# Layer norms behind the convolutions in channel layout, with their statistics sent through DRAM

## The chip, the cores and the metric

One core of one Trainium2 chip runs the whole program. The time is device time in microseconds (us) from the start to the end of one execution, median over the runs.

Engines in the listings: PE multiplies matrices (TensorE), DVE is the vector engine, ACT the scalar engine, POOL the GpSimd engine, SP the queue from which nearly all DMAs are issued. PE writes its results to PSUM, which has eight banks here; all other operands lie in SBUF. A DMA moves data between SBUF and DRAM.

## What is computed

One layer of a hybrid encoder, for a prompt of 512 tokens and a sample of 1024 tokens with shared weights. The part that the change touches is the layer norm behind the depthwise convolution:

```python
def _layernorm(x, g, b):
    mu = jnp.mean(x, axis=-1, keepdims=True)
    xc = x - mu
    return xc * lax.rsqrt(jnp.mean(xc * xc, axis=-1, keepdims=True) + EPS) * g + b
...
z = rmsnorm(x, norm_attn_g) @ w_in
a_out = window_attn(q, k, v, bias, band, sink)           # 8 heads of 64
c = ca * sigmoid(cb)                                     # 512 channels
c = dwconv(c, conv_dw_w, conv_dw_b)                      # 31 taps
c = silu(layernorm(c, conv_ln_g, conv_ln_b))             # mean over the 512 channels of a token
x = x + concat([a_out, c], axis=-1) @ w_out
...
```

What follows (a gated feed-forward network with a 3-tap convolution, and a last norm) isn't touched.

## The kernel before

Tokens are cut into blocks of 128: the prompt has blocks 0 to 3, the sample blocks 4 to 11. Every large product is done with operands split into a high and a low part, three matmuls of 128x512 per product (hi x hi, hi x lo, lo x hi); L317 to L319 are those of the projections, L813 to L815 those of the out projection, each with one line number for each of the three.

The projected channels lie with channels on the 128 partitions and tokens along the row, so that the convolution can shift along the tokens. The 512 channels are four chunks. The layer norm wants the mean over channels, which here lie across partitions. `conv_norm(i)` (L744) therefore turns each block: four PE transposes (L760) bring it to 128 tokens x 512 channels in a PSUM bank, `bn_stats` and `bn_aggr` (L765, L766) on DVE give mean and variance of each token, two small operations on POOL (L147, L148) make rstd of the variance, one DVE operation (L769) subtracts and multiplies with a value per partition, and four more PE transposes (L775) bring the block back. Then ACT applies g and b per channel (L781, four activations of 128x128), tanh (L782), DVE finishes the swish (L783), and ACT and DVE make the high and low parts (L784, L785) that the out projection reads as kc 4 to 7. The attention's half of the concatenation is kc 0 to 3. `out_half(i, n)` (L803) does block i's out projection, half n, in a PSUM bank, with kc 0 to 7 in order.

For the prompt, `prompt_attention` goes through the attention units 0 to 7 (two per block; `scores` with L655 to L676, `values` with L697 to L723) and does the norm of block u - 4 behind unit u. All chunks of the convolution are kept in SBUF (`kept`). `prompt_out` waits for each block through the set `ready`. For the sample, the convolution's result went through DRAM (`cvd`) and each block is read back into `held`; the norms of blocks 4 and 5 run inside `sample()` next to the feed-forward network of the prompt, and those of blocks 6 to 11 after it.

What sets the order: the code is written as generators that are advanced in turn at paces (`pace`, `side`), and a scheduler then orders the instructions on each engine, which executes its queue strictly in order. Buffers are named slots (`Slots`): letters h, q, d, c, s for SBUF, a, u, b, c for PSUM banks, and a new tile takes the slot that was freed first among the smallest that fit, so a change in one place gives other slots, and other waits, further on. From about 733 us on the order is written out by hand; the change doesn't reach there.

Other lines that the prediction uses: L407 to L433 (`evac`) empty the projections' PSUM banks on DVE, L433 for q, L407 for the convolution's gate; L435 and L438 make the low part of q and write both parts to DRAM (`qsd`), from where they are read back (h<-qsd); L659 is the softmax's first step on DVE, L700, L721 and L723 make low parts and sums of the attention on DVE and POOL, L699, L719 and L720 copy from PSUM on ACT; L983 (DVE), L1005 (DVE) and L1007 (SP, write to gap) belong to the feed-forward network beside it; L152 loads rows of x, and L1116 loads norm_ffn_g to all partitions.

## Time and profile before

| | |
|---|---|
| median of 3 runs | 1481.91 us (1481.87 to 1482.33) |
| profiled execution | 1484.05 us |
| its span on the core | 1482.1 us |
| mean granted clock of PE | 0.998 |
| instructions | 19791 |
| DVE, ACT, POOL busy | 75%, 54%, 54% |

The profile is of one execution. A row of the timeline gives the start, the length, the engine, the line, the tiles written and read and, in brackets, how long the engine had been idle and what released it. Matmuls are pipelined: one of 128x512 takes 0.39 us but they start 0.23 us apart, so a row's length is no cost by itself; the distance between starts is. A group's row gives the busy time and the mean of one, then the idle time ahead of its instructions with its releasers. A row of DMA issues gives the size of one in KB and the median time from issue to landing.

### The profile page before, as it was taken

What the parts mean: (1) busy time and instruction counts of PE and PEld (TensorE: products, weight loads), DVE (VectorE), ACT (ScalarE), POOL (GpSimd) and SP (SyncE); (2) the same over time, 40 slices, a digit from 0 to 9 for tenths busy, and PEclk for the clock granted to TensorE, in tenths of its full rate; (3) what the DMA queues carried; (4) which work ended last, traced back from release to release, by engine and by line L of the source; (5) the groups of instructions that cost most, each with busy time, mean ns of one, the idle gap of its engine ahead of it and who ended that gap; (6) DMA issues with size and microseconds to landing.
All of it is one profiled execution on the core that took longest, in us unless ns stands there. A gap on an engine that the chain in (4) does not pass through costs nothing.

```text
span 1482.1 us, 19791 instructions
## 1 busy us (share of the span) xinstructions
PE 1464.6 (99%) x6688; PEld 1206.0 (81%) x6688; DVE 1117.9 (75%) x1502; ACT 805.8 (54%) x1434; POOL 803.8 (54%) x696
## 2 busy tenths in 40 slices
PE   9999999999999999999999999999999999999998
PEld 7788887878888888788887888888888888888886
DVE  6877945658998989666598888888886846578873
ACT  7534555458778677644565445444454553433355
POOL 3555453328888776422566666666655341135555
PEclk9999999999999999999999999999999999999999
DMA  9555331744444464373214433333333494356744
GB/s 368 191 152 145 110 101 36 244 161 142 122 142 135 136 192 136 110 282 123 84 58 142 150 129 127 131 124 123 123 126 96 147 337 152 125 190 220 228 166 156
DMA packets 124625, 228.17 MB, mean 154 GB/s; under 512 B 20420, under 2 KB 45764, under 8 KB 124397
## 3 DMA queue, kind: packets, MB, share of 16 engines
q1 hardware_dynamic: 124092, 226.37, 46.4%
q8 instruction: 52, 0.85, 0.2%
q10 hardware_dynamic: 432, 0.56, 0.1%
q14 instruction: 49, 0.39, 0.1%
HBM read 166.83 MB, written 61.10 MB: 154 GB/s over the span
## 4 chain that ended last, share of the span: by engine, by line
PE 88%; DVE 4%; DMA 2%; ACT 2%; issue 2%; POOL 1%; SPq 0%; POOLq 0%; ACTq 0%; DVEq 0%
PE w L1249 8%; PE w L1250 8%; PE w L1251 8%; PE w L1613 7%; PE w L1614 7%; PE w L1612 7%; PE b L317 4%; PE u L317 4%; PE b L318 4%; PE u L318 4%; PE u L319 4%; PE b L319 4%; PE a L655 1%; PE a L697 1%; PE u L813 1%
## 5 line engine op out<-in xcount | busy, mean ns | idle before, releaser
L164 POOL TENSOR_TENSOR q<-q,q 128x1024 fp32r<-128x1024 f32 x64 | 154.4, 2413 | 69.4 <-ACT q L163 48.7
L1102 POOL TENSOR_TENSOR q<-q,q 128x512 fp32r<-128x512 f32 x82 | 125.4, 1538 | 115.2 <-ACT q L1235 115.2
L1102 DVE TENSOR_TENSOR h<-h,h 128x512 fp32r<-128x512 f32 (+1 forms) x161 | 132.6, 854 | 55.9 <-ACT h L1110 23.7
L1612 PE MATMUL w<-h,h 128*128 128x512 f32 x432 | 168.0, 389 | 0.0
L1614 PE MATMUL w<-h,h 128*128 128x512 f32 x432 | 168.0, 389 | 0.0
L1613 PE MATMUL w<-h,h 128*128 128x512 f32 x412 | 160.3, 389 | 0.0
L1102 POOL TENSOR_TENSOR h<-h,h 128x512 fp32r<-128x512 f32 (+1 forms) x46 | 67.9, 1478 | 141.7 <-ACT h L1595 119.6
L1249 PE MATMUL w<-h,q 128*128 128x512 f32 x350 | 137.7, 393 | 1.1 <-ACT w L1320 0.9
L1251 PE MATMUL w<-h,q 128*128 128x512 f32 x350 | 136.4, 390 | 0.1
L1250 PE MATMUL w<-h,q 128*128 128x512 f32 x350 | 136.3, 389 | 0.0
L1110 ACT CAST h<-h 128x512 fp32r<-128x512 f32 x116 | 69.2, 620 | 106.0 <-DVE h L1102 30.5
L317 PE MATMUL b<-h,q 128*128 128x512 f32 x312 | 123.2, 395 | 1.5 <-ACT h L466 0.9
L318 PE MATMUL b<-h,q 128*128 128x512 f32 x312 | 122.8, 393 | 0.0
L319 PE MATMUL b<-h,q 128*128 128x512 f32 x312 | 122.6, 394 | 0.0
L317 PE MATMUL u<-h,q 128*128 128x512 f32 x272 | 107.3, 395 | 0.8 <-DVE h L983 0.8
L319 PE MATMUL u<-h,q 128*128 128x512 f32 x272 | 107.2, 394 | 0.0
L318 PE MATMUL u<-h,q 128*128 128x512 f32 x272 | 107.2, 394 | 0.0
L357 DVE SCALAR_TENSOR_TENSOR c<-d,cvw,c 128x512 f32<-128x512 f32 x128 | 95.8, 749 | 1.5
L163 ACT CAST q<-q 128x1024 fp32r<-128x1024 f32 x66 | 69.0, 1046 | 49.0 <-PE b L318 13.3
L1612 PEld LDWEIGHTS w<-h,h 128*128 128x128 f32 x432 | 81.1, 188 | 16.9
L1614 PEld LDWEIGHTS w<-h,h 128*128 128x128 f32 x432 | 81.1, 188 | 16.6
L348 POOL TENSOR_TENSOR h<-h,h 128x512 f32<-128x512 f32 x62 | 82.1, 1326 | 20.9 <-ACT h L347 16.6
(501 smaller groups left out, 4011.1 us busy)
## 6 DMA issues: line engine op xcount, KB each, us to landing
q<-in_laid_w_up SPq DMA_DIRECT2D x88, 512.0 KB, 3.8
ga<-q SPq DMA_DIRECT2D x65, 256.0 KB, 2.2
h<-gap SPq DMA_DIRECT2D x57, 256.0 KB, 3.8
h<-ga SPq DMA_DIRECT2D x57, 256.0 KB, 3.5
h<-in_w_down SPq DMA_DIRECT2D x52, 256.0 KB, 3.5
q<-in_laid_w_in SPq DMA_DIRECT2D x22, 512.0 KB, 4.0
gap<-h SPq DMA_DIRECT2D x42, 256.0 KB, 2.6
q<-in_x_sample SPq DMA_DIRECT2D x15, 512.0 KB, 7.7
```

What stands on the lines that cost most here:

```text
L164: (nc.vector if dve else nc.gpsimd).tensor_tensor(lo[:], raw[:], hi[:].bitcast(F32), op=ALU.subtract)
L317: nc.tensor.matmul(out, whi[:, kc, :], hi[:], start=(kc == 0), stop=False)
L318: nc.tensor.matmul(out, whi[:, kc, :], lo[:], start=False, stop=False)
L319: nc.tensor.matmul(out, wlo[:, kc, :], hi[:], start=False, stop=(kc == KC - 1))
L357: nc.vector.scalar_tensor_tensor(acc[:], src(t), w(t), acc[:], op0=ALU.mult, op1=ALU.add)
L1102: (eng or nc.vector).tensor_tensor(out, a, b, op=ALU.subtract)
L1249: nc.tensor.matmul(out, whi[:, s], hi[:], start=(start and c == 0), stop=False, **go)
L1250: nc.tensor.matmul(out, whi[:, s], lo[:], start=False, stop=False, **go)
L1251: nc.tensor.matmul(out, wlo[:, s], hi[:], start=False, stop=(stop and c == 3), **go)
L1612: nc.tensor.matmul(out, sh[:, c], th[:], start=(p == 0 and not seeded), stop=False, **go)
L1613: nc.tensor.matmul(out, sh[:, c], tl[:], start=False, stop=False, **go)
L1614: nc.tensor.matmul(out, sl[:, c], th[:], start=False, stop=(p == NPAIR - 1), **go)
```

## The change

The turn back goes away. Blocks stay in channel layout, and only the statistics, one mean and one rstd per token, are brought to a form that can be applied there: a row along the tokens, the same on all partitions.

For a block of the sample the four transposes for the statistics stay. rstd is made in place beside the mean (`spread_stats`), both are written to a small DRAM tensor `lnd` (2 x 128 values, in single elements), and a second DMA reads them back broadcast to all partitions (128 x 256). DVE subtracts the mean's row from the block as loaded (128x512, `held`), POOL multiplies with the rstd's row, and ACT reads that in place of the PSUM bank.

For the prompt the norms of all four blocks are done together, behind unit 4: 16 transposes, four times `bn_stats` and `bn_aggr`, one rstd for all (128 x 4), one write of 128 x 8 values to `pstat`, and two broadcast reads of 128 x 512. Then the work goes by channel chunks, 512 tokens at a time: chunks 0 and 1 behind unit 5, 2 and 3 behind unit 6, each with a subtraction on DVE, a multiplication on POOL, and the same operations as before on whole chunks (one activation in place of four). The out projection reads slices of the chunks (`Chunks`). The four blocks become ready together, behind unit 6.

In the core of the diff, line numbers shift: transposes for the statistics are L769 in the changed kernel (L913 for the prompt), the write and the read of `lnd` L748 and L750, the prompt's subtractions L929, and L832 to L834 are what L813 to L815 were.

```diff
@@ -741,6 +741,15 @@
         for L in range(2):
             nc.sync.dma_start(cats[i, 0][L][:].bitcast(F32), catd[blocks[i][1], :, L, :].rearrange("p (j t) -> p j t", t=P))
 
+    lnd = [dr.tile([2, P], F32, name=f"lnd{b}") for b in range(8)]
+
+    def spread_stats(b, mv):
+        rstd_of(mv[:, 1:2], 1.0, mv[:, 1:2])
+        nc.sync.dma_start(lnd[b][:].rearrange("s p -> p s"), mv[:])
+        wide = sb.tile([2, P])
+        nc.sync.dma_start(wide[:], lnd[b][:].partition_broadcast(P))
+        return wide
+
     def conv_norm(i):
         G, b = blocks[i]
         if G["g"] == 0:
@@ -760,25 +769,35 @@
             nc.tensor.transpose(pt[:, c * P:(c + 1) * P], cv[c], ident[:])
         if G["g"] == 0 and b == G["nb"] - 1:
             kept.clear()
-        held = None
-        st, mv, rs = sm(6), sm(2), sm(1)
+        st, mv = sm(6), sm(2)
         nc.vector.bn_stats(st[:], pt[:])
         nc.vector.bn_aggr(mv[:], st[:])
-        rstd_of(mv[:, 1:2], 1.0, rs[:])
-        xh = sb.tile([CCH])
-        nc.vector.tensor_scalar(xh[:], pt[:], mv[:, 0:1], rs[:], op0=ALU.subtract, op1=ALU.mult)
-        del pt
-        for _ in range(YN):
-            yield 0.0
-        p2 = bank("norm")
-        for c in range(4):
-            nc.tensor.transpose(p2[:, c * P:(c + 1) * P], xh[:, c * P:(c + 1) * P], ident[:])
+        if G["g"] == 1:
+            del pt
+            wide = spread_stats(b, mv)
+            for _ in range(YN):
+                yield 0.0
+            nc.vector.tensor_tensor(held[:], held[:], wide[:, 0:1, :].to_broadcast([P, 4, P]), op=ALU.subtract)
+            nc.gpsimd.tensor_tensor(held[:], held[:], wide[:, 1:2, :].to_broadcast([P, 4, P]), op=ALU.mult)
+            del wide
+            p2 = held[:].rearrange("p c t -> p (c t)")
+        else:
+            rs, xh = sm(1), sb.tile([CCH])
+            rstd_of(mv[:, 1:2], 1.0, rs[:])
+            nc.vector.tensor_scalar(xh[:], pt[:], mv[:, 0:1], rs[:], op0=ALU.subtract, op1=ALU.mult)
+            del pt
+            for _ in range(YN):
+                yield 0.0
+            p2 = bank("norm")
+            for c in range(4):
+                nc.tensor.transpose(p2[:, c * P:(c + 1) * P], xh[:, c * P:(c + 1) * P], ident[:])
         y, t = sb.tile([4, P]), sb.tile([4, P])
         for c in range(4):
             o, n = y[:, c, :], p2[:, c * P:(c + 1) * P]
             if G["g"] == 1:
                 o, n = o.rearrange("p (k h) -> p h k", h=2), n.rearrange("p (h k) -> p h k", h=2)
             nc.scalar.activation(o, n, AF.Identity, scale=lng[:, c:c + 1], bias=lnb[:, c:c + 1])
+        held = None
         nc.scalar.activation(t[:], y[:], AF.Tanh)
         nc.vector.scalar_tensor_tensor(t[:], t[:], 1.0, y[:], op0=ALU.add, op1=ALU.mult)
         nc.scalar.copy(cat[0][:], t[:])
@@ -882,13 +901,64 @@
     use.update(step="b", turn="a", attn="au", norm="au", out="u", gate="b")
 
     ready = set()
-
-    def normed(i):
-        yield from conv_norm(i)
-        ready.add(i)
+    pstat = dr.tile([4, 2, P], F32, name="pstat")
+    wides = []
+
+    def prompt_stats():
+        drain(convs)
+        mv = sm(8)
+        for b in range(4):
+            pt = bank("norm")
+            for c in range(4):
+                nc.tensor.transpose(pt[:, c * P:(c + 1) * P], kept[c][:, b * P:(b + 1) * P], ident[:])
+            st = sm(6)
+            nc.vector.bn_stats(st[:], pt[:])
+            nc.vector.bn_aggr(mv[:, 2 * b:2 * b + 2], st[:])
+            del pt
+            yield 0.0
+        var = mv[:].rearrange("p (b s) -> p b s", s=2)[:, :, 1]
+        nc.gpsimd.tensor_scalar(var, var, 1.0, EPS, op0=ALU.mult, op1=ALU.add)
+        nc.gpsimd.tensor_tensor(var, var, nhalf[:], op=ALU.pow)
+        nc.sync.dma_start(pstat[:].rearrange("b s p -> p (b s)"), mv[:])
+        for s in range(2):
+            wides.append(sb.tile([4, P]))
+            nc.sync.dma_start(wides[s][:], pstat[:, s, :].partition_broadcast(P))
+
+    def prompt_norm(c):
+        x = kept.pop(c)
+        nc.vector.tensor_tensor(x[:], x[:], wides[0][:].rearrange("p b t -> p (b t)"), op=ALU.subtract)
+        nc.gpsimd.tensor_tensor(x[:], x[:], wides[1][:].rearrange("p b t -> p (b t)"), op=ALU.mult)
+        yield 0.0
+        hi, lo, t = sb.tile([NT], F32R), sb.tile([NT], F32R), sb.tile([NT])
+        nc.scalar.activation(x[:], x[:], AF.Identity, scale=lng[:, c:c + 1], bias=lnb[:, c:c + 1])
+        nc.scalar.activation(t[:], x[:], AF.Tanh)
+        nc.vector.scalar_tensor_tensor(t[:], t[:], 1.0, x[:], op0=ALU.add, op1=ALU.mult)
+        nc.scalar.copy(hi[:], t[:])
+        nc.vector.tensor_tensor(lo[:], t[:], hi[:].bitcast(F32), op=ALU.subtract)
+        for i in range(4):
+            for full, part in zip(cats.setdefault((i, 1), (Chunks(i), Chunks(i))), (hi, lo)):
+                full.parts.append(part)
+        yield 0.0
+
+    class Chunks:
+        def __init__(self, i):
+            self.parts, self.cols = [], slice(i * P, (i + 1) * P)
+
+        def __getitem__(self, at):
+            return self.parts[at[1]][:, self.cols]
+
+    def in_turn(*gens):
+        for gen in gens:
+            yield from gen
+
+    def all_ready():
+        wides.clear()
+        ready.update(range(4))
+        yield 0.0
 
     def prompt_attention():
-        yield from attention(0, 8, {u: normed(u - 4) for u in range(4, 8)})
```

Three places in the order. Names are kind of slot, slot number and a running number; "h41_1051" is a tile in SBUF slot h41, "c0_343" one in PSUM bank c0.

The first is DVE in the prompt's part, around units 4 to 6. Before, from the evacuation of q (L433, bank b0_91) on:

```order
L433 SCALAR_TENSOR_TENSOR h34_358_2223<-b0_91_2163,d1_125_569 128x512
L765 BN_STATS s18_352_2194<-a2_92_2189 128x6
L700 TENSOR_TENSOR d0_339_2095<-u1_87_2089,h35_338_2094 128x512
L670 RECIPROCAL s17_325_2011<-s17_325_2011 128x4
L766 BN_AGGR s19_353_2195<-s18_352_2194 128x2
L700 TENSOR_TENSOR h30_344_2127<-u0_90_2121,h38_343_2126 128x512
L659 ISA h29_367_2266,s21_365_2261<-u1_95_2263,q11_186_1099,nsink_81 128x256
L659 ISA s21_365_2261 128x1
L407 TENSOR_TENSOR d0_371_2314<-b1_94_2252,h0_109_467 128x512
L721 TENSOR_TENSOR h38_349_2158<-a1_88_2098,h36_331_2061 64x512
L700 TENSOR_TENSOR q10_375_2339<-u1_101_2333,q4_374_2338 128x512
L407 TENSOR_TENSOR q7_378_2374<-b0_100_2326,d1_125_569 128x512
```

and in the changed kernel, directly behind the four blocks' statistics and an L721 that writes h38_349; L433 with bank b0_91 is again the evacuation of q, h14_361 is the broadcast row of the means, and L407 with b1_95 empties the bank that b1_94 was:

```order
L659 ISA d0_370_2323,s23_364_2285<-u1_100_2320,q12_187_1101,nsink_81 128x256
L659 ISA s23_364_2285 128x1
L659 ISA h32_366_2290,s23_364_2285<-a1_97_2287,q11_186_1099,nsink_81 128x256
L659 ISA s23_364_2285 128x1
L700 TENSOR_TENSOR q9_372_2348<-u0_102_2342,h44_371_2347 128x512
L433 SCALAR_TENSOR_TENSOR h38_355_2233<-b0_91_2172,d1_125_569 128x512
L700 TENSOR_TENSOR q10_374_2363<-a1_103_2357,q4_373_2362 128x512
L929 TENSOR_TENSOR h2_83_354<-h2_83_354,h14_361_2279 128x512
L929 TENSOR_TENSOR h27_141_744<-h27_141_744,h14_361_2279 128x512
L929 TENSOR_TENSOR h17_198_1177<-h17_198_1177,h14_361_2279 128x512
L929 TENSOR_TENSOR h26_291_1817<-h26_291_1817,h14_361_2279 128x512
L407 TENSOR_TENSOR h38_368_2311<-b1_95_2255,h0_109_467 128x512
```

L433 moved from ahead of the first statistics to behind the softmax steps L659 and two low parts; its tile h38_355 takes the slot that the POOL sum behind L721 (h38_349) frees. The four subtractions stand ahead of L407. The row of L659 with only a sum as its output fetches the accumulated sum of the one before.

The second is PE at block 5 of the sample. Before: the turn back (L775) of block 5, and its first use as h13 and h56 in bank u1_349:

```order
L813 MATMUL u1_349_6600<-h21_1005_6093,h15_1063_6418 128x512
L814 MATMUL u1_349_6600<-h31_1006_6094,h15_1063_6418 128x512
L815 MATMUL u1_349_6600<-h21_1005_6093,h46_1064_6419 128x512
L775 MATMUL c0_343_6498<-ident_82,h48_1075_6455 128x128 x4
L813 MATMUL u0_350_6674<-h23_1102_6623,h57_1037_6262 128x512
L814 MATMUL u0_350_6674<-h20_1103_6624,h57_1037_6262 128x512
...
L813 MATMUL b0_352_6730<-h40_1106_6650,h15_1063_6418 128x512
L814 MATMUL b0_352_6730<-h39_1107_6651,h15_1063_6418 128x512
L813 MATMUL u1_349_6600<-h58_1012_6125,h13_1065_6422 128x512
L814 MATMUL u1_349_6600<-h10_1013_6126,h13_1065_6422 128x512
L815 MATMUL b0_352_6730<-h40_1106_6650,h46_1064_6419 128x512
```

and in the changed kernel: the transposes for the statistics, and the first use of the normed rows, h41 and h13, in bank c0_343:

```order
L712 MATMUL a1_336_6428<-q11_1057_6396,h60_431_2734 128x512
L769 MATMUL c0_334_6405<-ident_82,h43_1053_6386 128x128 x4
L711 MATMUL a1_336_6428<-q12_1061_6424,h60_431_2734 128x512
...
L834 MATMUL b0_347_6745<-h21_992_6058,h26_1107_6651 128x512
L769 MATMUL a2_348_6758<-ident_82,h58_1120_6735 128x128 x4
L832 MATMUL b1_349_6797<-h25_1087_6582,h29_1106_6650 128x512
L833 MATMUL b1_349_6797<-h46_1088_6583,h29_1106_6650 128x512
L769 MATMUL a0_345_6660<-ident_82,h33_1105_6648 128x128 x4
L834 MATMUL b1_349_6797<-h25_1087_6582,h26_1107_6651 128x512
L832 MATMUL c0_343_6559<-h54_999_6090,h41_1051_6384 128x512
L833 MATMUL c0_343_6559<-h8_1000_6091,h41_1051_6384 128x512
```

Between the last transposes of the block and its first use stood 42 rows before, all behind the turn back; now 48 rows lie between the statistics' transposes and the use, with the subtraction, the activations and the rest of the norm beside them on the other engines.

The third is SP in the same stretch of the changed kernel, from the load of block 6's convolution on. lnd1 is block 5's, lnd2 and lnd3 those of blocks 6 and 7, and in_norm_ffn_g is the load that L1116 issued before (L1186 now):

```order
L762 DMA h33_1105_6648<-cvd_159 128x512
L748 DMA lnd1_1273<-s30_1059_6411 128x2x1
L1077 DMA gap24_3279<-q11_1069_6490 128x512
L152 DMA q1_1141_6853<-in_x_sample 128x1024
L750 DMA q3_1060_6417<-lnd1_1273 128x256
L152 DMA q11_1124_6743<-in_x_sample 128x1024
L1186 DMA q3_1070_6496<-in_norm_ffn_g 128x1024
L748 DMA lnd3_1275<-s8_1126_6764 128x2x1
L748 DMA lnd2_1274<-s4_1109_6666 128x2x1
L750 DMA h32_1127_6770<-lnd3_1275 128x256
L152 DMA q14_1155_6949<-in_x_sample 128x1024
L750 DMA h59_1110_6672<-lnd2_1274 128x256
```

Before, there were no writes of statistics and no reads of them; the loads and the gap write stood there alone. Now the read of lnd1 stands behind the write to gap24 and a load of x, and the writes of blocks 6 and 7 stand behind the load of norm_ffn_g.

More of the change, by code (lines that the diff above doesn't have):

```diff
@@ L890, in prompt_attention @@
+    class Chunks:
[10 more added lines that the diff above has]
+        yield 0.0
     def prompt_attention():
-        yield from attention(0, 8, {u: normed(u - 4) for u in range(4, 8)})
+        yield from attention(0, 8, {4: prompt_stats(), 5: in_turn(prompt_norm(0), prompt_norm(1)),
+                                    6: in_turn(prompt_norm(2), prompt_norm(3), all_ready())})
```

## The prediction, on record before the changed kernel was timed

> **What bounds the kernel now.** First the page, for the engines and the chain that ended last:
>
> ```profile
> PE 1464.6 (99%) x6688; PEld 1206.0 (81%) x6688; DVE 1117.9 (75%) x1502; ACT 805.8 (54%) x1434; POOL 803.8 (54%) x696
> PE 88%; DVE 4%; DMA 2%; ACT 2%; issue 2%; POOL 1%; SPq 0%; POOLq 0%; ACTq 0%; DVEq 0%
> ```
>
> TensorE (PE) is busy 99% of the span and carries 88% of the chain: a microsecond of matmul taken away is a microsecond won, as long as PE doesn't have to wait for something new. Then the windows over the stretch in which the change reorders PE, about 217 to 731 us. The columns are window, length, busy time of PE, PEld, DVE, ACT and POOL (with counts), granted clock, DMA share, GB/s:
>
> ```profile
> 216.70:226.40 9.70, 9.55 (x49) 7.95 (x48) 5.32 (x13) 5.06 (x12) 4.36 (x7) 1.00 0.67 189
> 237.00:251.00 14.00, 12.92 (x69) 10.18 (x68) 10.33 (x22) 10.04 (x22) 5.15 (x10) 1.00 0.01 2
> 276.80:300.00 23.20, 22.88 (x104) 18.50 (x103) 14.47 (x21) 9.76 (x19) 8.03 (x8) 1.00 0.93 285
> 613.00:625.20 12.20, 9.86 (x48) 7.43 (x47) 8.53 (x15) 5.84 (x13) 2.33 (x6) 1.00 0.24 80
> 625.20:628.60 3.40, 3.39 (x9) 2.67 (x10) 3.37 (x9) 3.40 (x9) 0.19 (x1) 0.54 0.10 36
> 633.00:649.20 16.20, 16.20 (x80) 13.43 (x79) 11.06 (x19) 11.02 (x24) 2.98 (x4) 1.00 0.97 376
> 649.20:735.00 85.80, 85.80 (x418) 70.88 (x417) 51.49 (x66) 39.65 (x78) 36.99 (x43) 1.00 0.37 123
> ```
>
> From 633 us on PE has no idle time at all, and that is where blocks 5 to 11 of the sample are normed and projected. So each norm is hidden today, and the question is by how much. The stretch 613 to 625.2 has 2.3 us idle, and directly behind it the granted clock is 0.54 for 3.4 us.
>
> **What is removed.** Of the turn back, block 4's in the timeline of PE (start, length, instruction, what it waited for), with what follows:
>
> ```profile
> 620.62 0.60 PE L775 MATMUL c<-ident,h 128*128 128x128 f32 x4
> 620.98 0.48 PE L317 MATMUL u<-h,q 128*128 128x512 f32 x1
> 621.30 0.40 PE L318 MATMUL u<-h,q 128*128 128x512 f32 x1
> 621.54 0.40 PE L319 MATMUL u<-h,q 128*128 128x512 f32 x1
> 622.54 0.50 PE L655 MATMUL a<-q,h 128*128 128x256 f32 x2 [0.61 <-DVE h L721]
> ```
>
> Four transposes put the next matmul 0.36 us later, and that one delays its successor by 0.32 instead of the usual 0.23: 0.36 + 0.32 - 0.23 = 0.45 us. Twelve blocks: 12 x 0.45 = 5.4 us. This block's own four stand just ahead of a wait for DVE, whose end they don't set, so they win nothing: 4.95 us. The twelve tensor_scalars (L769) go from DVE, but as many subtractions come; DVE is off the path in all but the places below.
>
> **What is added: a round trip through DRAM for every block of the sample.** The rows for it, per issue in KB and us to landing, then groups with mean ns:
>
> ```profile
> qsd<-h SPq DMA_DIRECT2D x44, 128.0 KB, 2.4
> cvd<-h SPq DMA_DIRECT2D x8, 256.0 KB, 3.0
> h<-qsd SPq DMA_DIRECT2D x24, 256.0 KB, 3.1
> q<-in_norm_ffn_g SPq DMA_DIRECT2D x1, 512.0 KB, 7.0
> L723 POOL TENSOR_TENSOR h<-h,h 64x512 fp32r<-64x512 f32 x17 | 22.8, 1339 | 25.7 <-DVE h L721 25.4
> L148 POOL TENSOR_TENSOR s<-s,nhalf 128x1 f32<-128x1 f32 x12 | 8.6, 714 | 1.0
> ```
>
> The write of the statistics (256 elements of 4 bytes) is in no row of this kernel. Its nearest neighbours are 2.4 us (qsd) and 3.0 us (cvd, in runs of 256 bytes); I take 2.5. The broadcast read of 128 KB: below 2.4 hardly, 3.0 taken, 7.0 (the row of the broadcast norm_ffn_g, four times the bytes) as the far end, since the DMA share in its stretch is 0.97. *One rule speaks to this:* the Trainium skill, "DMA: Bandwidth & Descriptors", section "Anatomy of one DMA", has about 2.0 us fixed for each DMA plus bytes over 436 GB/s; the pair would be 4.3 us instead of 5.5, and the wait worked out below 1.2 us shorter, the sum +2.7 instead of +3.9. The rows above land later than that for small transfers, so I go by the rows.
>
> Blocks 6 to 11 have 16 to 25 us between their statistics and their first use by PE in the new order (counted at 0.23 us a matmul), against a chain of some 15 us with its queues: I put no stall there. **Block 5 is the exception.** In the new order its statistics stand 38 matmuls, eight transposes of L697 and two groups of four ahead of the first matmul that reads its normed rows (c0 with h41): 38 x 0.23 + 0.8 + 2 x 0.45 = 10.4 us. Before, the turn-back at 643.5 stood 10.0 us ahead of that use (here the first row is the statistics' transposes, the last the use), and behind it was only this chain:
>
> ```profile
> 636.92 0.60 PE L760 MATMUL c<-ident,h 128*128 128x128 f32 x4
> 643.50 0.68 DVE L1005 TENSOR_TENSOR q<-b,q 128x512 f32<-128x512 f32 x1
> 644.14 1.52 ACT L781 ACTIVATE q<-c,vecs 128x128 f32<-128x128 f32 x4 [2.97 <-PE c L775]
> 646.70 0.58 ACT L719 COPY h<-a 64x512 f32<-64x512 f32 x1
> 647.30 0.63 ACT L782 ACTIVATE q<-q 128x512 f32<-128x512 f32 x1
> 648.00 0.68 DVE L783 SCALAR_TENSOR_TENSOR q<-q,q 128x512 f32<-128x512 f32 x1
> 649.09 0.62 ACT L784 CAST h<-q 128x512 fp32r<-128x512 f32 x1
> 649.55 1.28 POOL L723 TENSOR_TENSOR h<-h,h 64x512 fp32r<-64x512 f32 x1 [5.80 <-DVE h L721]
> 649.74 1.64 DVE L785 TENSOR_TENSOR h<-q,h 128x512 fp32r<-128x512 f32 x1 [0.33 <-ACT h L784]
> 653.53 0.39 PE L813 MATMUL u<-h,h 128*128 128x512 f32 x1
> ```
>
> Laid out on the times of before: the statistics' transposes stand six matmuls later than at 636.92, and end at 638.7; bn_stats and bn_aggr, behind one tap in DVE's queue, to 641.2; the two small POOL operations 0.95 to 642.15; write 2.5 to 644.75; on SP the read stands behind a gap write, which before was issued at 644.20 behind the evacuation L1005, so it leaves at 644.8; read 3.0 to 647.8; subtraction 0.7; multiplication on POOL 1.34; four activations 1.5; tanh 0.65; two copies of the attention ahead in ACT's queue 1.1 (L719 and its like); the DVE product lies beside them; cast 0.65: 653.85. PE asks at 638.7 + 10.4 = 649.1. **Stall: 4.7 us.** If every queue were empty it is 2.7; with the read at 7.0 it is 8.7. Behind the waiting cast and the waiting read stand the copies and casts of later blocks on ACT, and on SP the x loads and the reads of blocks 6 and 7, which have the slack just named.
>
> After such a stall I expect the clock drop seen at 625.2: 3.4 us at 0.54 cost 3.4 x 0.46 = 1.6 us. It came there behind 2.3 us of idle time in several pieces; the 1.1 us idle in 237 to 251 left the clock at 1.00. So 4.7 us should be enough, and 1.6 us is the term (0 is the other end).
>
> **What is moved in the prompt.** All four blocks' statistics are now taken after unit 4, in one bunch, and the rows of DVE that follow are in another order:
>
> ```profile
> 219.59 0.69 DVE L433 SCALAR_TENSOR_TENSOR h<-b,d 128x512 f32<-128x512 f32 x1
> 226.98 1.24 SPq L438 DMA_DIRECT2D qsd<-d  x2
> 230.10 0.69 DVE L407 TENSOR_TENSOR d<-b,h 128x512 f32<-128x512 f32 x1 [3.79 <-DMA qsd<-d]
> ```
>
> L433, which empties bank b0, ran at 219.59 with slack. Now it takes a slot that L723 frees, and stands behind L659, which writes the d slot that the two qsd writes hold until 230.1 less some tenths. L659 twice, one L700 and L433 itself bring it to about 231.7, while PE, which from the last statistics (226.9) to the projection that wants b0 has 2.0 us of work, asks at 228.9: **2.75 us** of stall (2.0 to 3.3). Then the round trip: statistics done 227.9, POOL 1.0, write 3.0, read 3.1, so 235.1. Four subtractions and L407, which empties bank b1, take 5 x 0.69, to 238.6; PE asks for b1 24 matmuls and one score after 231.9, at 237.7: 0.9 us. But the subtractions read two SBUF tensors while POOL multiplies, and L785 above took 1.64 instead of about 0.69 where it met L723; with two such meetings of 1 us it is 2.9. I take **1.9 us**. *This is the second rule:* the Trainium skill, "SBUF — State Buffer", section "SBUF: two separate sides", calls the port pair of the two engines an exclusive lock held for the whole instruction; by it alone the term is 2.9, without it 0.9, and the row at 649.74 agrees with the lock. On the other side the turn of units 6 and 7 with the old waits goes: idle time 0.15 + 1.08 + 0.32 in the first three windows, and some four restarts at 0.39 - 0.23 = 0.16 each, 2.1 us, of which only L775's part, 0.3, is sure.
>
> **The sum**: -4.95 + 2.75 + 1.9 - 2.1 + 4.7 + 1.6 = +3.9 us. The profiled execution took 1484.05 us (span 1482.1 and 1.95 around it), so 1487.95 for a run like it; that execution was 2.1 us above the median of 1481.91, which gives **1485.8 us** for the median.
>
> **The rivals.** (a) *The round trips hide* (0.20): queues are emptier than I laid out, block 5's wait falls to below 2.7 without a clock drop and the prompt's stalls to those that go. Then the 4.95 us stand with 0 to 2 us off: 1477.0 to 1478.9, faster. For it: PE's order was laid out so that operands should be there, and in 85.8 us behind 649.2 it never waits today. Against: DMAs of before land 2.4 to 7.0 us after issue and the chain has four engines. (b) *The two sides cancel* (0.28): block 5 waits about 3 us, the clock stays, the prompt gives back what it loses: -4.95 + 0.9 + 3.0 = -1.0, so 1479 to 1484.8. (c) *The forecast* (0.38): 1484.9 to 1489. (d) *Far slower* (0.14): the read waits at the crowded DMA (7.0), or a second clock drop follows the prompt's two stalls (1.6 more), or block 6 or 7 comes late behind block 5's read on SP: 8.7 in place of 4.7 and 1.6 more is +9.5, 1489 to 1493. The deciding point between (a) and (c) is one number: the time from the last transposes of block 5's statistics to its cast; under 12 us it is (a), at 15 it is the forecast. That the 48 transposes don't go is no rival: they are not in the new program.
>
> **The numbers.** What a measurement can tell from no change is about 0.2%, 3 us: faster is under 1478.9, slower above 1484.9. Faster 0.20, same 0.28, slower 0.52. The range takes in (b), (c), half of (a) and most of (d): 1478.0 to 1491.0. The likeliest sign's own range is 1484.9 to 1491.
>
> **What would show it.** Right: in the new trace the matmul of L832 on c that first reads block 5's rows waits some 4 to 5 us for ACT's cast, with a window of granted clock about 0.54 behind it; near 229 a matmul L317 waits on L433, and near 237 one on L407; no L775 is left and PE's busy time is about 5 us less. Wrong: PE without idle time behind 630 us, statistics' writes that land in 2 us and under, or a wait of 8 us or more at block 5; and if blocks 6 to 11 stall, their slack was counted too high.

## The result, and the profile after

| | before | changed |
|---|---|---|
| median, us | 1482.12 (4 runs, 1481.87 to 1482.39) | 1555.17 (4 runs, 1552.64 to 1558.93) |
| ratio to before | | 1.0493, 95% interval 1.0473 to 1.0513 |
| profiled execution, us | 1484.05 (span 1482.1) | 1558.93 (span 1557.1) |
| mean granted clock of PE | 0.998 | 0.974 |

Slower, as forecast, but by 73 us where the forecast said 4, and far outside the range. The engines on the page of the changed kernel:

```profile
PE 1479.2 (95%) x6640; PEld 1215.2 (78%) x6640; DVE 1121.8 (72%) x1502; ACT 803.9 (52%) x1422; POOL 816.2 (52%) x702
```

PE does 48 instructions less and is busy 14.6 us longer (1479.2 against 1464.6), at a mean granted clock of 0.974 in place of 0.998; and it is idle 77.9 us (1557.1 - 1479.2) where it was idle 17.5 before. 60.4 us more idle time and 14.6 us more busy time make the 75.0 us between the two spans. The windows of the changed kernel say where (window, length, busy time of PE, PEld, DVE, ACT and POOL, granted clock, DMA share, GB/s):

```profile
226.40:262.00 35.60, 23.53 (x90) 18.70 (x91) 15.83 (x27) 14.22 (x29) 15.79 (x15) 0.76 0.15 38
262.00:620.00 358.00, 354.73 (x1686) 295.11 (x1685) 288.64 (x509) 247.92 (x457) 233.72 (x210) 1.00 0.50 150
620.00:700.00 80.00, 51.64 (x216) 40.64 (x215) 33.56 (x62) 30.69 (x65) 16.67 (x22) 0.82 0.51 138
700.00:760.00 60.00, 50.32 (x205) 40.27 (x204) 21.50 (x30) 15.76 (x31) 13.40 (x20) 0.88 0.51 113
760.00:812.00 52.00, 38.52 (x164) 30.65 (x163) 23.76 (x27) 20.53 (x40) 25.68 (x23) 0.84 0.22 67
```

One stretch behind the prompt's statistics with 12.1 us idle, and the whole stretch of the sample's norms with 28.4 + 9.7 + 13.5 us. In both the granted clock is 0.76 to 0.88; in between it is 1.00 and PE is busy 354.73 of 358 us. The DMA issues of the two round trips come next (KB each, median us to landing):

```profile
lnd<-s SPq DMA_DIRECT2D x8, 1.0 KB, 8.8
pstat<-s SPq DMA_DIRECT2D x1, 4.0 KB, 10.5
h<-lnd SPq DMA_DIRECT2D x7, 128.0 KB, 4.8
```

One kilobyte takes 8.8 us to land, longer than the half megabytes of the weights (3.7 for q<-in_laid_w_up). And the waits of PE between 215 and 830 us (who waited for whom, us in total, times, longest):

```profile
PE u L1202 <- ACT h L1215: 11.2, 1, 11.2
PE b L317 <- DVE h L407: 10.3, 1, 10.3
PE c L832 <- ACT h L803: 9.5, 1, 9.5
PE a L655 <- DVE h L721: 8.5, 2, 7.3
PE u L833 <- DVE h L869: 6.9, 1, 6.9
PE a L769 <- DMA h<-cvd: 6.8, 2, 3.6
PE b L832 <- ACT h L803: 4.6, 2, 2.8
PE u L832 <- ACT h L803: 3.6, 1, 3.6
```

L803 is the cast that makes a block's normed rows. Only the waits for it, 17.7 us in three rows, are waits for the norm. The others are for other work: a low part of the attention (L721), of w_out (L869), a transposed block for the next stage (L1215), the evacuation of a bank (L407), a load (cvd). How L721 comes to be late is seen in the timeline of the changed kernel:

```profile
626.85 0.37 SPq L748 DMA_DIRECT2D lnd<-s  x1
629.65 0.68 DVE L1075 TENSOR_TENSOR d<-b,h 128x512 f32<-128x512 f32 x1
635.06 0.32 SPq L750 DMA_DIRECT2D h<-lnd  x1
639.95 0.69 DVE L780 TENSOR_TENSOR q<-q,h 128x512 f32<-128x512 f32 x1 [9.62 <-DMA h<-lnd]
641.34 0.69 DVE L721 TENSOR_TENSOR h<-a,h 64x512 f32<-64x512 f32 x1
642.09 0.80 PE L655 MATMUL a<-q,h 128*128 128x256 f32 x2 [7.29 <-DVE h L721]
```

The write of block 4's statistics leaves at 626.85; the read, which waits for it on SP, at 635.06; the subtraction L780 holds DVE from 630.3 to 639.95, and behind it in DVE's queue stands L721, for which PE stands still.

Three more of the waits have the same form. L869 stands on DVE behind the L780 of another block, which waited 9.85 us for its row; L407 stands behind the prompt's subtractions L929, which waited 11.56 us for h<-pstat; and L1215, the longest, stands on ACT behind the activation L799 of a normed block, whose row came late:

```profile
783.47 0.69 DVE L780 TENSOR_TENSOR h<-h,h 128x512 f32<-128x512 f32 x1 [11.63 <-DMA h<-lnd]
785.59 1.65 ACT L799 ACTIVATE h<-h,vecs 128x128 f32<-128x128 f32 x4 [14.48 <-POOL h L781]
787.26 0.58 ACT L1215 COPY h<-u 128x512 f32<-128x512 f32 x1
787.90 1.12 PE L1202 MATMUL u<-ident,q 128*128 128x128 f32 x4 [11.18 <-ACT h L1215]
```

These four make 11.2 + 10.3 + 7.3 + 6.9 = 35.7 us of PE's waits, twice those for normed rows.

### The profile page after: what moved, and what is told of

It is laid out like the page before. It is cut to its first block, busy times and chain, and to the rows that moved or that the text cites. A ratio compares the mean times of both kernels' runs of the same rounds, so it can differ in the third digit from the quotient of the medians.

```text
span 1557.1 us, 19711 instructions
## 1 busy us (share of the span) xinstructions
PE 1479.2 (95%) x6640; PEld 1215.2 (78%) x6640; DVE 1121.8 (72%) x1502; ACT 803.9 (52%) x1422; POOL 816.2 (52%) x702
## 4 chain that ended last, share of the span: by engine, by line
PE 47%; DMA 7%; DVE 2%; POOL 2%; issue 1%; ACT 1%; SPq 0%; POOLq 0%; ACTq 0%; DVEq 0%
PE w L1319 9%; PE w L1320 8%; PE w L1321 8%; PE w L1684 6%; PE w L1682 6%; PE w L1683 6%; DMA lnd<-s 4%; DMA h<-lnd 2%; DVE q L1172 1%; PE b L833 0%; PE b L834 0%; PE b L832 0%; DMA h<-in_laid_w_out 0%; POOL q L1762 0%; POOL q L1172 0%
## 5 line engine op out<-in xcount | busy, mean ns | idle before, releaser
L1172 DVE TENSOR_TENSOR h<-h,h 128x512 fp32r<-128x512 f32 (+1 forms) x161 | 136.0, 876 | 55.1 <-ACT h L1180 21.6
L1172 POOL TENSOR_TENSOR h<-h,h 128x512 fp32r<-128x512 f32 (+1 forms) x46 | 68.6, 1495 | 138.4 <-ACT h L1665 108.3
L317 PE MATMUL b<-h,q 128*128 128x512 f32 x312 | 124.8, 401 | 11.6 <-DVE h L407 10.3
L318 PE MATMUL b<-h,q 128*128 128x512 f32 x312 | 124.1, 398 | 0.0
L319 PE MATMUL b<-h,q 128*128 128x512 f32 x312 | 123.9, 397 | 0.0
L317 PE MATMUL u<-h,q 128*128 128x512 f32 x272 | 107.7, 397 | 0.3 <-DVE h L1053 0.3
L348 POOL TENSOR_TENSOR h<-h,h 128x512 f32<-128x512 f32 x62 | 82.0, 1325 | 21.7 <-ACT h L347 17.4
```

The costliest lines, as they stand in the source:

```text
L317: nc.tensor.matmul(out, whi[:, kc, :], hi[:], start=(kc == 0), stop=False)
L318: nc.tensor.matmul(out, whi[:, kc, :], lo[:], start=False, stop=False)
L319: nc.tensor.matmul(out, wlo[:, kc, :], hi[:], start=False, stop=(kc == KC - 1))
L1172: (eng or nc.vector).tensor_tensor(out, a, b, op=ALU.subtract)
```

## The experiments

Thirteen kernels beside the changed one. Times are medians; a ratio is to the kernel before, run beside it on the same chip.

**One half of the change at a time.** The prompt's norms of before with the sample's of the changed kernel, and the other way round:

```diff
-        yield from attention(0, 8, {4: prompt_stats(), 5: in_turn(...), 6: in_turn(...)})
+        yield from attention(0, 8, {u: normed(u - 4) for u in range(4, 8)})     # sample_only
...
-        if G["g"] == 1:
+        if False:                                                               # prompt_only
```

> The change for the sample alone; the prompt's norms as before. Of the 73 us lost, the stalls of PE in the changed kernel before 340 us make some 18 and those behind 620 us some 70 (by starts of matmuls, clock included). Theory A: about 1482 + 55 to 60 = 1537 to 1542 us. If the two parts hang together through the order, it is somewhere else.

> The change for the prompt alone; the sample's norms as before. One write (10.5 us to landing) and one pair of reads, waited for once. Theory A: 1482 + 12 to 18 = 1494 to 1500 us, all of it as idle time of PE between 225 and 255 us and a clock drop behind.

Measured: 1541.37 us (ratio 1.0401, 1.0380 to 1.0422) and 1497.40 us (1.0104, 1.0084 to 1.0124). Both fit: 59 and 15 us add up to about the 73 of the whole, so the two halves lose by themselves. In prompt_only PE is idle 10.8 of the 30 us between 225 and 255 us, at a granted clock of 0.77; behind that the clock is 1.00.

**The write by itself.** Scratch writes behind the last output, each followed by a read that has to wait for it:

```diff
+    trip("el2", sc["el2"][:].rearrange("s p -> p s"), w[:, 0:2], 256)      # 256 values, as in the change
+    trip("run2", sc["run2"][:], w[:, 0:2], 256)                            # 128 pairs
+    trip("row512", sc["row512"][:], w[0:2, 0:P], 256)                      # 2 rows of 512 bytes
+    trip("own", sc["own"][:, 0:2], w[:, 0:2], 256)                         # 128 pairs, 512 bytes apart
+    trip("run8", sc["run8"][:], w[:, 0:8], 1024)                           # 128 runs of 32 bytes
...
```

> The kernel before, with eleven writes to scratch DRAM added behind its last output, each followed by a broadcast read of what it wrote, so that every one runs alone in a quiet machine. Nothing of the computation is left out; the time is longer by the added DMAs and is not compared. Theory A (the form of the write costs): 256 elements of 4 bytes land in about 8 us as in the changed kernel (7.8 to 10.5 there), 128 rows of 512 bytes and 2 rows of 512 bytes in 2 to 2.5 us. If it is the number of pieces, 128 pieces of 8 bytes take about half of the extra, and 1024 pieces four times as much; if it is that pieces share a stretch of DRAM, the 128 pieces of 8 bytes that lie 512 bytes apart are fast. Theory B (the writes of the changed kernel were late because of what ran beside them): all of them land in 2 to 3 us here.

From SP's timeline; L1852 is a write and the L1854 behind it the read that waits for its landing, so the distance of their starts is the write's time:

```profile
1486.92 0.37 SPq L1852 DMA_DIRECT2D sc_el<-c  x1
1494.78 0.32 SPq L1854 DMA_DIRECT2D c<-sc_el  x1
1499.51 0.32 SPq L1852 DMA_DIRECT2D sc_run<-c  x1
1502.92 0.32 SPq L1854 DMA_DIRECT2D c<-sc_run  x1
...
1517.58 0.25 SPq L1852 DMA_DIRECT2D sc_row<-c  x1
1518.70 0.33 SPq L1854 DMA_DIRECT2D c<-sc_row  x1
...
1523.13 0.32 SPq L1852 DMA_DIRECT2D sc_own<-c  x1
1524.54 0.32 SPq L1854 DMA_DIRECT2D c<-sc_own  x1
```

256 single values take 7.9 us in an idle machine, the same kilobyte as 128 pairs 3.4, as two rows 1.1; and 128 pairs that lie 512 bytes apart 1.4. (Of the three rows of sc_el, for 256, 128 and 1024 single values, the first is shown.) 128 runs of 32 bytes took 1.4, 1024 single values 10.5, as in the prompt. So it isn't, in the main, what ran beside them (theory B falls), nor the number of pieces, but that pieces lie close together. How close, the next kernel asks:

```diff
+    trip(1, flat[1][0:2 * P].rearrange("(p e) -> p e", e=2)[:, 0:1], col)   # e = 1, 2, 4, 8, 16 words apart
+    trip(6, flat[6][0:P].rearrange("(j i o) -> i j o", j=16, o=1), col)     # neighbours from other partitions
...
```

> The kernel before with eleven more scratch writes behind its last output, each again alone; nothing of the computation is left out, the time isn't compared. In the first series 128x1 values next to each other landed in 6.8 us, 128x2 in 3.4, 128x8 and 128 pairs 512 bytes apart in 1.4. Theory A1 (pieces that share a short stretch of DRAM are written one after another): single values at a distance of 8, 16, 32 and 64 bytes take about 3.4, 2, 1.4 and 1.4 us, so that the time follows the number of values in a stretch of 32 bytes, not the number or size of pieces. Then two permuted places of the 128 values, where neighbours in DRAM come from partitions 8 or 16 apart: if only pieces that one DMA engine writes in a row collide, one of them is fast (1.4 to 2 us); if any pieces do, both stay near 6.8. Theory A2 (small pieces are slow in themselves): all single values take 6 us or more wherever they lie.

Measured the same way (L1856 is the write, L1857 the read), here for 128 single values 4 bytes apart and 32 bytes apart:

```profile
1486.44 0.33 SPq L1856 DMA_DIRECT2D sc<-c  x1
1494.09 0.32 SPq L1857 DMA_DIRECT2D c<-sc  x1
...
1511.17 0.32 SPq L1856 DMA_DIRECT2D sc<-c  x1
1512.58 0.32 SPq L1857 DMA_DIRECT2D c<-sc  x1
```

Single values 4, 8, 16, 32 and 64 bytes apart: 7.7, 3.0, 2.0, 1.4 and 1.4 us; 16-byte runs side by side 2.0; the two permuted orders of single values 7.7 and 6.6. Theory A1 fits in every row: eight, four, two or one piece in 32 bytes take about 7, 3, 2 and 1.4 us, whichever partitions they come from. The Trainium skill, "DMA: Bandwidth & Descriptors", section "Specifications", has a read-modify-write for transfers below 512 bytes; the rows agree only in part: some writes below that size are dear, but 128 runs of 32 bytes are as fast here as rows of 512 bytes (1.4 against 1.1 to 1.5 us).

**A fast write in the kernel.** First the statistics turned into rows of 512 bytes by PE, then laid out in pairs as they lie in SBUF:

```diff
-        nc.sync.dma_start(lnd[b][:].rearrange("s p -> p s"), mv[:])
+        nc.tensor.transpose(pt[0:2, 0:P], mv[:], ident[:])         # rows_512
+        nc.scalar.copy(row[0:2, :], pt[0:2, 0:P])
+        nc.sync.dma_start(lnd[b][:], row[0:2, :])
...
+        nc.sync.dma_start(lnd[b][:], mv[:])                        # pair8: lnd[b] is [P, 2]
```

> The changed kernel, but a PE transpose turns the statistics (128x2, in the prompt 128x8) into rows, ACT copies them from PSUM, and the write moves 2 (8) runs of 512 bytes in place of 256 (1024) elements of 4 bytes. Theory A: the write lands in 2 to 2.5 us in place of 7.8 to 10.5, so the kernel is where the price of 2.5 us had put it, 1480 to 1490 us. Theory B (queues and busy DMA): the writes still land in 6 us or more and the time stays above 1530 us.

> The changed kernel, with the statistics laid out in DRAM as they lie in SBUF: 128 pieces of 8 bytes for a block of the sample, 128 of 32 bytes for the prompt, no step more on any engine, and the subtraction and multiplication read the rows with a stride. Theory A: writes land in 3.4 and 1.4 us (first series), reads as before; that is within 1 us of the prices of the prediction, so its other terms are tested: about 1486 us by the prediction's sum, up to 1495 if the reads' 3.8 to 4.8 us and the wait of each read on SP add 1 to 1.5 us for most of the eight trips. Theory C (it is the number of trips in a row on SP, each held by its wait, and not the 8 us of the write): above 1510.

Measured: 1504.04 us (1.0151, 1.0134 to 1.0168) and 1507.97 us (1.0178, 1.0161 to 1.0195). About 50 of the 73 us are the form of the write; but neither kernel came to the 1480 to 1495 expected, and pair8 lies just under the 1510 from which theory C, the number of trips in a row, was to hold. In rows_512 PE itself now waits 5.1 us for POOL's rstd at the new transpose (L748), in its own queue. In pair8 DVE's waits for the reads are about half of what they were in the changed kernel, 38.9 us against 70.8:

```profile
DVE h L780 <- DMA h<-lnd: 25.8, 5, 7.9
DVE h L780 <- DMA q<-lnd: 8.8, 1, 8.8
DVE q L780 <- DMA h<-lnd: 4.3, 1, 4.3
```

PE's longest wait in pair8 is still the one for block 5. Its write leaves at 639.82, beside loads of x and a gap write, the read only 5.8 us later:

```profile
639.82 0.33 SPq L748 DMA_DIRECT2D lnd<-s  x1
645.65 0.32 SPq L750 DMA_DIRECT2D q<-lnd  x1
...
656.22 0.80 PE L832 MATMUL c<-h,h 128*128 128x512 f32 x1 [9.54 <-ACT h L803]
```

**No one waits for the write.** The reads take a constant row, so the norm works with ones in place of mean and rstd; once with the writes still issued, once without them:

```diff
-        nc.sync.dma_start(wide[:], lnd[b][:].partition_broadcast(P))
+        nc.sync.dma_start(wide[:].rearrange("p s t -> p (s t)"), lnflat[0:2 * P].partition_broadcast(P))
...
-        nc.sync.dma_start(lnd[b][:].rearrange("s p -> p s"), mv[:])     # const_nowrite alone
```

> The changed kernel, except that the broadcast reads take a constant row of ones, written to DRAM at the start, in place of the statistics: the statistics are made and written as before, but no one waits for them, and the norm uses the constants. Theory A (the loss is waiting for the round trip): all but a few us of the 73 go, 1478 to 1486 us; 48 transposes less are worth 5 us, the prompt's new order costs up to 5. If the writes' traffic or SP's time were the loss, it would stay above 1500.

> The kernel that read constant rows, with the writes of the statistics left out too (the statistics are still made; the norm uses ones). It took 1520 us with the writes, though no one waited for them. Theory D (a slow write holds up the DMAs beside it on the same queues, so that loads and the attention's trips land late): without the writes the rest goes, 1478 to 1486 us, and catd<-h, 7.2 us to landing there and 2.0 before, is back near 2 to 3. Theory E (the loss there is the new order: reads early in SP's queue, subtractions early in DVE's): it stays above 1505 us.

1519.65 us (1.0254, 1.0234 to 1.0275) with the writes, 1487.56 us (1.0039, 1.0023 to 1.0055) without. The first was a miss that mattered: with no one waiting, 38 us stayed, and 32 of them went with the writes. Two things go with a write: the time in which it is under way, and the time for which it stands on SP until its statistics are there, with SP's later DMAs behind it (17.4 us for the eight in const_read). How the 32 us are shared between the two wasn't separated. What a write under way does is seen among the DMAs that were issued between 660 and 680 us in const_read:

```profile
q<-in_x_sample SPq DMA_DIRECT2D x3, 512.0 KB, 10.7
catd<-h SPq DMA_DIRECT2D x2, 256.0 KB, 11.5
gap<-q SPq DMA_DIRECT2D x1, 256.0 KB, 12.2
lnd<-s SPq DMA_DIRECT2D x2, 1.0 KB, 12.0
```

All that was issued in this stretch took 8 to 12 us (two groups aren't shown). Before the change, between 600 and 780 us, in_x_sample took 4.3, gap<-q 5.6 and catd<-h 2.0; without the writes catd<-h takes 2.3. The same by itself, a probe of 256 KB behind a small write:

```diff
+    phase(0, None, rd, nc.sync)     # the probe alone
+    phase(1, el2, rd, nc.sync)      # behind 256 single values
+    phase(2, run8, rd, nc.sync)     # behind 128 runs of 32 bytes
...
```

> The kernel before with nine phases of scratch DMAs behind its last output; nothing is left out of the computation and the time isn't compared. In each phase a probe of 256 KB (a read, or a write) is issued on SP right behind a small write of 256 single values (slow, 7.9 us alone) or of 128 runs of 32 bytes (1.4 us), or alone; once the probe goes ahead of the small write, and twice it is issued from ACT's queue. Theory D: alone the probe lands in 2 to 4 us, behind the slow write in 8 to 10 us, behind the fast one in 2 to 4. If only DMAs of the same issuing queue are held, the probe from ACT stays fast. Theory E: the probe lands in 2 to 4 us everywhere.

Alone a read lands in 2.6 us and a write in 2.0. Behind the single values, issued 2.2 to 2.6 us after them, the read takes 5.7 and the write 7.7, so both land at or behind the end of the slow write. Behind the 32-byte runs the write again takes 2.0. Theory D holds for one queue. The DMA engines have room all the while: the 272 packets of the slow write in m1_shapes all lie in its first 2 us, and from 1488.9 to its landing at 1494.8 the trace shows no packet at all; and the packets of the 256 KB write behind the slow one are over 1.9 us after its issue, 5.8 us before it lands. (Those of the read are spread over nearly all of its 5.7 us.)

Two forms stay open, since their landings aren't in the trace: the probe ahead of the slow write, and the probe on ACT's queue behind it. For the second the packets say a part. ACT's queue shows its last ones 4.6 to 5.0 us after the issue, about 1 us before the slow write's landing, where behind the fast write that probe landed in 2.8 us. So, as far as the packets show, it was late but did not wait for the end of the slow write.

**Fast writes and more room.** Two of four words per token (16 bytes, 2.0 us in the series above; the read of a block grows to 256 KB with it, and POOL clears the words first), 32 bytes in the prompt, and more pauses between statistics and subtraction, which by the count in the order give every block 17 us or more where block 5 had 10.3:

```diff
-YN = 2
+YN = 3                                                             # quad16_yn4: 4
...
-    lnd = [dr.tile([2, P], F32, name=f"lnd{b}") for b in range(8)]
+    lnd = [dr.tile([P, 4], F32, name=f"lnd{b}") for b in range(8)]
```

> The changed kernel with 16 bytes a token in DRAM (two of four words used; 2.0 us to write in the second series) for the sample, 32 bytes a token for the prompt, and three in place of two pauses of the generator between statistics and subtraction, after which the shortest time between statistics and use on PE, counted in the order, is 18.4 us for any block of the sample (10.3 in the changed kernel). If block 5's short distance and the slow write are the causes: 1477 to 1483 us. If the round trips hold one another through the queues of DVE and SP whatever their distance: 1490 to 1505.

> The same with four pauses; the shortest distance is 17.2 us, block 5's 25.4. Same expectations as with three: 1477 to 1483 us if distance and write are the causes, 1490 to 1505 if the trips hold one another.

1501.02 us (1.0133, 1.0116 to 1.0150) and 1503.76 us (1.0145, 1.0128 to 1.0161): the rival's range. The write lands in 1.4 and 1.9 us in the median (5.2 and 4.2 at most), and still DVE stands at L781, the subtraction, with L721 behind it. From quad16_yn3's timeline:

```profile
619.99 0.32 SPq L750 DMA_DIRECT2D q<-lnd  x1
...
624.95 1.06 DVE L781 TENSOR_TENSOR q<-q,q 128x512 f32<-128x512 f32 x1 [6.15 <-issue]
626.04 0.69 DVE L721 TENSOR_TENSOR h<-a,h 64x512 f32<-64x512 f32 x1
626.79 0.79 PE L655 MATMUL a<-q,h 128*128 128x256 f32 x2 [7.32 <-DVE h L721]
```

The profile gives no releaser for L781 ("issue"), but the read of block 5's row lands 4.9 us after its issue, at 624.9, just when L781 starts. The pauses of the generator have not put enough of DVE's work ahead of the subtraction. So the last edit on the sample takes it off DVE:

```diff
-            nc.vector.tensor_tensor(held[:], held[:], wide..., op=ALU.subtract)
+            nc.gpsimd.tensor_tensor(held[:], held[:], wide..., op=ALU.subtract)
```

> The kernel with 16 bytes a token and three pauses (1501 us), with the sample's subtraction on POOL in front of its multiplication, so that nothing on DVE waits for a round trip. In that kernel DVE stood 6 us at a subtraction with the attention's L721 behind it, for which PE then waited 7.3 us. Theory F (what is left of the loss is other work that stands on DVE behind a subtraction that waits): most of the 19 us goes, 1482 to 1490 us. If the normed rows themselves come too late, or the wait moves to POOL, where L723 of the attention stands: 1497 to 1505.

1504.39 us (1.0152, 1.0137 to 1.0168): no gain, and theory F falls as it was put. The trace shows such a wait one engine further on. POOL's product is late, ACT's activation L800 waits for it, and the attention's copies L719 and L720 stand behind L800:

```profile
619.82 1.65 ACT L800 ACTIVATE h<-q,vecs 128x128 f32<-128x128 f32 x4 [7.64 <-POOL q L782]
621.50 0.58 ACT L719 COPY h<-a 64x512 f32<-64x512 f32 x1
622.09 0.58 ACT L720 CAST h<-a 64x512 fp32r<-64x512 f32 x1
...
622.70 0.69 DVE L721 TENSOR_TENSOR h<-a,h 64x512 f32<-64x512 f32 x1 [7.10 <-ACT h L720]
...
623.45 0.69 PE L655 MATMUL a<-q,h 128*128 128x256 f32 x2 [4.71 <-DVE h L721]
```

This wait isn't new. In quad16_yn3 it stood at the same place, hidden behind DVE's longer one:

```profile
619.83 1.65 ACT L800 ACTIVATE h<-q,vecs 128x128 f32<-128x128 f32 x4 [6.89 <-POOL q L782]
```

So with DVE free L721 starts 3.3 us earlier (622.70 in place of 626.04) and no more. PE's wait for L721 fell from 7.3 to 4.7 us, others came. An order in which DVE, POOL and ACT all take up a block's second half only when its row has landed wasn't tried.

**The prompt with a fast write**, the sample as before:

```diff
-        nc.sync.dma_start(pstat[:].rearrange("b s p -> p (b s)"), mv[:])
+        nc.sync.dma_start(pstat[:], mv[:])                                # pstat is [P, 8]
...
+        nc.sync.dma_start(wides[0][:], pstat[:].partition_broadcast(P))
```

> The change for the prompt alone, its statistics written as 128 runs of 32 bytes (1.4 us to landing) and read with one broadcast of 512 KB; the sample's norms as before. The prompt alone with single values took 1497. Theory A and D: the write's 9 us and what it held up go, 16 turn-back transposes less win 1.8 us, and the prompt's stalls are then about those of before: 1479 to 1483 us, so equal to or a little faster than before. If the prompt's new order itself costs the 5 us that the prediction gave it: 1485 to 1488.

1482.47 us, 11 runs; ratio 1.0005, 0.9996 to 1.0014: no difference that can be measured. Beside prompt_only's 1497 it says that the 15 us of the prompt's loss went with the form of the write (the edit also makes one read, 3.3 us, of two, 3.9 us each). PE's waits for L407, 8.7 us in prompt_only, are gone. It is the best of the variants, and none beats the kernel before.

## Why the prediction was wrong

- **The step that failed is the price of the write**, "I take 2.5" (3.0 in the prompt), on which the 4.7 us at block 5 and the 1.9 us in the prompt rest. It was worked out from the nearest rows by size and packet, qsd (2.4) and cvd (3.0). Those move 128 to 256 KB in pieces of 256 bytes and more; what the new write has and they don't is eight pieces in each 32 bytes. It measured 8.8 us (10.5 in the prompt). The text said that the write was in no row of the kernel, and yet gave it no end above 3.0, while the read got one at 7.0. An operation that the trace doesn't show has no upper bound from rows that lack its property. The rule that the prediction quotes beside it doesn't bound it either: the Trainium skill, "DMA: Bandwidth & Descriptors", gives the 2.0 us plus bytes under "Anatomy of one DMA" for DMAs issued from GpSimd, and 1 KB issued from SP took 1.1 to 7.9 us here, by its form.
- **The write was charged only to those who wait for it.** Of the 38 us that const_read still lost with no one waiting, 32 went with the writes (const_nowrite): the other DMAs that a slow write holds up, and SP, where a write stands for its statistics. No term or rival had this.
- **The cost of a wait was taken at the wrong place.** The prediction asked when PE wants a block's rows, found slack for blocks 6 to 11 and didn't speak of block 4. It listed what stands behind the waiting cast on ACT and the read on SP, but not what stands on DVE behind the subtraction, nor on ACT behind the first activation. Block 4's trip held L721 for 7.3 us, and the four waits of that form make 35.7 us against 17.7 for normed rows; 8.2 of the 17.7 are outside block 5, so slack was counted too high as well. With the write made fast 19 to 26 us still remain (quad16_yn3, rows_512, pair8). Their longest waits of PE are of both kinds: 7.3 us for L721 in quad16_yn3, 9.5 for block 5's rows and 8.8 for L1214, which is L1215 of the changed kernel, in pair8, 5.1 for rstd in rows_512; how the 19 to 26 us split between them wasn't taken apart. So a fast write alone would not have made the forecast right; it would still have been five to seven times too small.
- **Block 5** was named rightly: the matmul L832 on bank c waits for ACT's cast L803, 9.5 us in place of 4.7, past the 8 us that the prediction gave as a sign of being wrong. From the statistics' transposes to the end of the cast it took 23.7 us (659.4 to 683.1) in place of 15.2; the write's 10.5 us in place of 2.5 are most of that. PE's wait isn't longer still because PE came 3.8 us later than laid out, 14.2 us behind the transposes in place of 10.4: ahead of the use it had stood 3.55 us at an L769 for a load (h<-cvd) that was under way together with the slow write. 4.7 + 8.5 - 3.8 is 9.4. In pair8 PE came 10.4 us behind the transposes, as laid out, and still waited 9.5, since beside loads of x and a gap write the write took 5.8 us (3.4 alone) and the read 4.3. So the layout of the chain held there, and its two DMAs, beside others, were priced too low.
- **The reads** landed in 4.8 us in place of 3.0, a mis-sized term inside its range.
- **The clock**: right in kind, and one drop of 1.6 us was counted. The table of waits alone has five stalls of about 7 to 11 us, and PE's busy time rose by 14.6 us in all, where 5 us less were forecast.
- **The prompt**: the wait of L317 on L407 came, at 10.3 us in place of 1.9, because of the write; that on L433 didn't come at b0, but PE waited 2.2 us in the attention's steps ahead of it (226.6 to 230.4). The four subtractions beside POOL's products took 4.65 us where 4 x 0.69 had been laid out, which is nearly the two meetings of 1 us that the prediction weighed. With the fast write the prompt's sum is 0 (prompt_run32), against +0.75 by the prediction's terms (2.75 + 1.9 - 2.1 less four blocks at 0.45). The 2.1 is 2.2 by its own numbers, and 2.5 us from 642.15 is 644.65; no other slip of the sums is larger.
- **The 5 us of the transposes** can't be read from any of the runs alone; const_nowrite, in which no one waits for statistics, is 5.8 us above the kernel before. There the loss is mostly in the prompt's stretch: from 215 to 270 us PE is idle 4.4 us at a granted clock of 0.91, where before it was idle 1.2 at 1.00, and the longest wait, 3.1 us, is for the statistics (bn_stats). In prompt_run32 that stretch has 2.6 us idle at 0.97; why the two differ wasn't followed.

So the direction was right, but for a small part of the reason, and for the rest by luck. The account from the runs: 1555.2 to 1519.7 when no one waits for statistics, to 1487.6 when the slow writes go as well. Left out together with the writes is SP's wait for the statistics, so the last step isn't the slow landing alone.

## What to carry to other kernels

Price a small write to DRAM by how many of its pieces fall into one short stretch of memory, 32 bytes here, not by its bytes; where the trace has no such transfer, its cost is open upwards, and a scratch transfer behind the last output measures it in one run. A slow write is also paid by the DMAs beside it on its queue. And a new wait costs what stands behind it on its engine: ask for each engine along the new chain, DVE, POOL and ACT alike, what the next instruction is and who waits for that.

## What the runs showed of the hardware that was not expected

- Small pieces written by one DMA are slow when they share 32 bytes: 128 values of 4 bytes took 7.7, 3.0, 2.0, 1.4 and 1.4 us at a distance of 4, 8, 16, 32 and 64 bytes, and a permuted order of partitions changed little (6.6 and 7.7). Four times as many values, 1024 in place of 256, took a third longer (10.5 against 7.9).
- While such a write was under way, a DMA behind it from the same queue didn't land: 5.7 and 7.7 us in place of 2.6 and 2.0 in the quiet machine, up to 12.2 us beside others. The trace shows no packets for most of that time (none from 1488.9 to 1494.8 in m1_shapes), so the DMA share doesn't betray it.
- A broadcast read of 512 KB in 4 KB rows landed in 3.3 us (prompt_run32), no later than most of the 128 KB ones (medians 2.8 to 4.8).
